# Four small changes of order and places in a streaming hybrid layer: column loads called earlier, SP's queue in program order in the heads, a third buffer, and own places for a row scale

## The chip, the cores and the metric

The kernel runs on one core of one Trainium2 chip. The metric is the device time of one execution in microseconds (us). A core has a matrix engine (PE, with the loading of its weights shown as PEld), a vector engine (DVE), a scalar engine (ACT), GpSimd (POOL) and SyncE (SP), which here issues nearly all DMA transfers. Each engine works through its own instructions in order and waits for the others by semaphores.

## The reference

One streaming step of one layer, for 512 frames of a new stream and 64 frames of a running one (576 rows, width 2048). All numbers are float32.

```
hn   = rmsnorm(x, g_norm1)
q, k, v, gb, gc, hc = split(hn @ w_in)            # six blocks of 1024 columns
q, k = rmsnorm per head                            # 8 heads x 128
o_attn = stick_breaking(q, [cached k, k], [cached v, v])   # strictly causal
u      = gc * hc
o_conv = gb * (causal convolution of width 3 over [state, u])   # 8 groups x 128 channels
mix    = concat(rmsnorm(o_attn), rmsnorm(o_conv))
x      = x + mix @ w_out
h2     = rmsnorm(x, g_norm2)
y      = x + (silu(h2 @ w_gate) * (h2 @ w_up)) @ w_down
```

The outputs are y of both streams, their new keys and values, and their new convolution states.

## The kernel before

**Tiling.** Activations lie transposed: channels on the 128 partitions, the 576 rows in the free dimension, in two halves of 288. A float32 value is split into a high and a low part (`split`, L222: ACT casts the high part, L223; DVE subtracts it, L224), and each product is three matmuls of 128 x 128 by 128 x 288. A weight is loaded by SP into one of the two slots of the tile `raw_a` (L184, or L946 for the columns below), then split in the same way (L176 and L177, or L223 and L224).

**The pipeline of ticks.** `project` (L489) runs one projection of 128 output columns: 16 steps for each of two halves, and one call of `pipe.tick()` after each step. Side work is written as generators that are spawned into this pipeline; each `yield n` asks to be resumed n ticks later. So the text order of the program, on every engine, is set by the ticks. A scheduler may then still change the order within each engine; inside `tc.manual_schedule(engines={SP})` SP's instructions stay in program order. Before the change this mode is on only in the later part of the conv products (L1112).

**Heads.** `head(h)` (L794) runs the projections of q, k and v for one head. It loads the cached keys and values (cK L798, cV L799), and spawns their transposition (L790), the scores (z, L672), softmax-like steps on ACT and the stores of new keys (ktok, L704) and values (vtok, L779).

**x_sums** (L570) is spawned after head 0. For each of 8 pieces it loads two tiles of x (L584), scales them on ACT (L587, L588), adds and subtracts on DVE (L590 and L592 among them), splits the sums into `xs_out` (L223, L224), and stores them to `xs_dram` on SP (L581). Its yields add up to 74 ticks a piece. The sums are the operands of a seven-product scheme for 2 x 2 block products (seven products in place of eight), used in the conv units and later.

**The first two conv groups** (`conv_group`, L889, for g below STD = 2) use three plain projections each: gc, hc, gb. During these, `head_forms` (L519) makes the seven combinations ("forms") of the attention output, splits them (hf) and stores them (`form_dram`, L544). Before the last projection, gb of group 1, `call_columns(range(3))` asks for the first three column loads of the conv units: two into the slots of raw_a, one into raw_c. `conv_prepare(0, 1)` and `conv_prepare(0, 2)` then split the first (whl).

**The conv units** run seven products p_ for each unit in the order of the list `corder` (`conv_run`, L990 for the matmuls). Two of the products are kept: `kept` (L997) copies a PSUM bank to a tile `part` with ACT (L999), in the tags "ms", "t" or "acc". A finished result goes through `done`: for a unit of kind "o" (the output projection's attention half, over the forms) DVE adds the bank to x (L1007), for the others cv is scaled (L1013, L1015).

**The mixed values.** `put_mix` (L510) scales a group's conv output by its gain into `mx` (ACT L513, DVE L515), sums squares (L507, L508), and POOL stores mx to `mix_dram` (L517). mx lies in the tag "hl", which has two buffers.

**The row scale.** `group_scale` (L558) splits the summed squares (`sqg`, also in "hl"), adds over channels with two matmuls (ssg, L470 and L471), and calls `rsqrt_mean` (L457), whose intermediate tiles ms and t have the tags "ms" and "t" with one buffer each.

**The output units' start.** In `open_out` three generators are spawned: `load_rest` (loads x from xt_dram on SP, L1070), `state_out` (PE transposition L1080, cst on ACT L1082, two stores L1083 and L1084) and `group_scale`. The forms are loaded by `load_forms` (L1054).

The projection of the mixed values and the feed-forward part after that (`out_proj` and on) take most of the time and are not touched.

Of the kernel before, what the change touches and what calls it, by code (L numbers as in the profile page):

```python
# [10 lines left out]
F32 = mybir.dt.float32  # L11
F32R = mybir.dt.float32r
# [4 lines left out]
P = 128  # L17
# [3 lines left out]
HALF = T // 2  # L21
HALVES = ((0, HALF), (HALF, T))
# [17 lines left out]
STD = 2  # L40
# [54 lines left out]
def tile_hybrid_stream_step(  # L95
# [99 lines left out]
    def next_weight():  # L195
        i = pos[0]
        pos[0] += 1
        end = first_out if i < first_out else first_block
        while len(raws) < min(i + 2, end):
            load_weight()  # L200
        while len(ready) < min(i + 2, end):
            split_weight(nc.gpsimd if i == 2 else nc.vector)
        while len(raws) < min(i + 3, end):
            load_weight()
        out = ready[i]
        ready[i] = None
        return out
# [18 lines left out]
    def parts(name):  # L226
        t = tmp.tile([P, 2, HALF], F32R, tag="hl", name=name)
        return t[:, 0], t[:, 1]
# [145 lines left out]
    with tc.manual_schedule(engines={mybir.EngineType.Activation, mybir.EngineType.DVE, mybir.EngineType.SP}):  # L374
        raw, raw3, src = weight_raw(0)
# [78 lines left out]

    hpool.release()

    def rsqrt_mean(dst, src, n, width):  # L457
        ms = tmp.tile([P, HALF], F32, tag="ms", name="ms", bufs=1)[:, :width]
        y = tmp.tile([P, HALF], F32, tag="y", name="y")[:, :width]
        t = tmp.tile([P, HALF], F32, tag="t", name="t", bufs=1)[:, :width]  # L460
        nc.vector.tensor_scalar(out=ms, in0=src, scalar1=1.0 / n, scalar2=EPS, op0=ALU.mult, op1=ALU.add)
        nc.scalar.activation(out=y, in_=ms, func=AF.Ln)
        nc.scalar.activation(out=y, in_=y, func=AF.Exp, scale=-0.5)
        nc.vector.tensor_tensor(out=t, in0=y, in1=y, op=ALU.mult)
        nc.vector.scalar_tensor_tensor(out=t, in0=t, scalar=-0.5, in1=ms, op0=ALU.mult, op1=ALU.mult)
        nc.vector.scalar_tensor_tensor(out=dst, in0=t, scalar=1.5, in1=y, op0=ALU.add, op1=ALU.mult)
# [19 lines left out]
                                op0=ALU.mult)  # L486
    split_weight(nc.vector)

    def project(evac, banks=(None, None), defer=None):  # L489
        whi, wlo = next_weight()  # L490
        for bank, (a, b) in zip(banks, HALVES):
            if bank:
                ps = ps_z.tile([P, 512], F32, tag=bank, name="pjz")[:, :HALF]
            else:
                ps = ps_pj.tile([P, HALF], F32, tag="pj", name="pj")
            product(ps, whi, wlo, slice(0, P), x_two, KD, a // HALF)
            if defer is None:
                evac(ps, a, b)
            else:
                defer.append((evac, ps, a, b))  # L500

    def add_squares(acc, src, first):
        if first:
            nc.scalar.activation(out=acc, in_=src, func=AF.Square)
        else:
            sq = tmp.tile([P, HALF], F32, tag="sq", name="sqm")
            nc.scalar.activation(out=sq, in_=src, func=AF.Square)  # L507
            nc.gpsimd.tensor_tensor(out=acc, in0=acc, in1=sq, op=ALU.add)  # L508

    def put_mix(g, i, src, gcol, acc, first):  # L510

        t = tmp.tile([P, 2, HALF], F32R, tag="hl", name="mx")
        nc.scalar.activation(out=t[:, 0], in_=src, func=AF.Copy, scale=gcol)  # L513
        add_squares(acc, src, first)
        nc.vector.scalar_tensor_tensor(out=t[:, 1], in0=src, scalar=gcol, in1=t[:, 0].bitcast(F32),  # L515
                                       op0=ALU.mult, op1=ALU.subtract)
        nc.gpsimd.dma_start(out=mix_dram[i, g].rearrange("f p t -> p f t"), in_=t.bitcast(F32))  # L517
# [39 lines left out]

    def group_scale(acc, dst, rows_of):  # L558

        for a, b in HALVES:  # L560
            sh, sl = parts("sqg")
            split(sh, sl, acc[:, a:b])
            yield rows_of
            ss = channel_sums(sh, sl, a, b, "ssg")
            rsqrt_mean(dst[:, a:b], ss, 8 * P, HALF)
            yield rows_of

    acc_a = rpool.tile([P, T], F32, tag="R", name="acc_a", bufs=2)
# [1 line left out]
    def x_sums():  # L570


        raw = o_half[1][:, 2:4, :]
        four = raw.rearrange("p k (i t) -> p (k i) t", i=2)
        b11, b12, b21, b22 = (four[:, q, :] for q in range(4))
        stt, tt = nc.vector.scalar_tensor_tensor, nc.vector.tensor_tensor

        def put(two, names):
            split(xs_out[:, :, 0, :], xs_out[:, :, 1, :], two)
            for r, q in enumerate(names):  # L580
                nc.sync.dma_start(out=xs_dram[q, j].rearrange("f p t -> p f t"), in_=xs_out[:, r].bitcast(F32))  # L581

        for j in range(NP):
            nc.sync.dma_start(out=raw, in_=xt_dram[2 * j : 2 * j + 2].rearrange("k p t -> p k t"))  # L584
            yield 18
            ge, go = g1c[:, 2 * j : 2 * j + 1], g1c[:, 2 * j + 1 : 2 * j + 2]
            nc.scalar.activation(out=b11, in_=b11, func=AF.Copy, scale=ge)  # L587
            nc.scalar.activation(out=b22, in_=b22, func=AF.Copy, scale=go)  # L588
            yield 8
            stt(out=b11, in0=b12, scalar=ge, in1=b11, op0=ALU.mult, op1=ALU.subtract)  # L590
            yield 8
            stt(out=b12, in0=b12, scalar=ge, in1=b22, op0=ALU.mult, op1=ALU.subtract)  # L592
            yield 8
            put(four[:, 0:2, :], (0, 2))
            yield 8
            tt(out=b22, in0=b22, in1=b11, op=ALU.subtract)
            yield 8
            stt(out=b21, in0=b21, scalar=go, in1=b22, op0=ALU.mult, op1=ALU.subtract)
            yield 8
            put(four[:, 2:4, :], (3, 1))  # L600
            yield 8
        free_places.append(True)
# [191 lines left out]
    def head(h):  # L794
# [26 lines left out]
        project(v_evac, ("z2", None) if h == 0 else (None, None))  # L821
        pipe.spawn(values(h, st, Ev))

    for h in range(NH):
        head(h)
        if h == 0:
            pipe.spawn(x_sums())


    cstate = rpool.tile([P, 2, 2, NG], F32, name="cstate")  # L830
# [15 lines left out]
        nc.sync.dma_start(out=t.bitcast(F32), in_=xs_dram[q].rearrange("j f p t -> p j f t"))  # L846

    def open_units():
        cx = apool.tile([P, 1024 + UW], F32, tag="ob", name="cx")
        bt["s1"] = cx[:, :1024].rearrange("p (j c) -> p j c", c=P)  # L850
        bt["c"] = cx[:, 1024 : 1024 + UW - 2]

# [11 lines left out]
    def put_u(a, b, x, y):  # L864
        e = min(b, TP)
        nc.vector.tensor_tensor(out=u[:, a + 2 : e + 2], in0=x[:, : e - a], in1=y[:, : e - a], op=ALU.mult)
        if b > TP:
            nc.vector.tensor_tensor(out=u[:, TP + 4 :], in0=x[:, e - a :], in1=y[:, e - a :], op=ALU.mult)
# [19 lines left out]
    def conv_group(g):  # L888
        gates = []  # L889

        def evac_gc(ps, a, b):
            t = tmp.tile([P, HALF], F32, tag="sq", name="gcr")
            nc.vector.tensor_tensor(out=t, in0=ps, in1=R1[:, a:b], op=ALU.mult)
            nc.vector.tensor_tensor(out=t, in0=t, in1=R1[:, a:b], op=ALU.mult)
            gates.append(t)

        project(evac_gc)
        begin_u(g)
        project(lambda ps, a, b: put_u(a, b, ps, gates[a // HALF]))

        def evac_gb(ps, a, b):
            if not bt:
                open_b()
            if a == 0:
                end_u(g)
            t = tmp.tile([P, HALF], F32, tag="y", name="gbr")
            nc.vector.tensor_tensor(out=t, in0=ps, in1=R1[:, a:b], op=ALU.mult)
            put_o(g, a // HALF, t)

        if g == STD - 1:  # L910
            call_columns(range(3))
            for p_ in (1, 2):
                conv_prepare(0, p_)
        project(evac_gb)
# [11 lines left out]
    def call_columns(gone):  # L926
        cfree.extend(gone)
        while cwanted:
            n, c = cwanted[0]
            place = [q for q in cfree if c is not None or q < 2][:1]  # L930
            if not place:
                return
            cwanted.pop(0)
            q = place[0]
            cfree.remove(q)
            raw = bt["raw"] if q == 2 else raw_tile["A"][:, q, :]
            if c is None:
                d = CU[n][1]
                nc.sync.dma_start(out=raw.rearrange("p (k c) -> p k c", c=2 * P),
                                  in_=w_out[:AW, 2 * d * P : 2 * (d + 1) * P].rearrange("(k p) c -> p k c", p=P))  # L940
                v = raw.rearrange("p (j s h c) -> p j s h c", s=2, h=2, c=P)
                for c in range(2):
                    cregion[n, c] = q, v[:, :, 0, c, :], v[:, :, 1, c, :]
            else:
                c0 = cstart[c + 2 * (CU[n][0] == "b")] + CU[n][1] * P
                nc.sync.dma_start(out=raw.rearrange("p (k c) -> p k c", c=P),  # L946
                                  in_=w_in[:, c0 : c0 + P].rearrange("(k p) c -> p k c", p=P))
                v = raw.rearrange("p (j s c) -> p j s c", s=2, c=P)
                cregion[n, c] = q, v[:, :, 0, :], v[:, :, 1, :]
# [800 lines left out]
```

## Time and profile before

| | us |
|---|---|
| median of three runs | 2415.28 |
| the three runs | 2414.83, 2415.28, 2418.58 |
| the profiled execution's own time | 2414.43 |
| its span in the profile | 2412.7 |
| PE busy | 2377.6 (99%) |
| DVE busy | 1910.5 (79%) |
| ACT busy | 1166.6 (48%) |
| POOL busy | 294.6 (12%) |

A row of the timeline has the start of an instruction in us, its duration in us, the engine, the line of the program, the operation, what it writes <- what it reads, the shape, and how many of one kind follow each other (x24); in brackets stands how long the engine had been idle before it and what released it. SPq rows are transfers being issued; they have the time that the issuing took. A row of the windows has the stretch, its length, the busy time and number of instructions of PE, PEld, DVE, ACT and POOL, then the granted PE clock as a share of full speed, the mean busy share of the 16 DMA engines (it can read a little over 1), and GB/s. A row of the groups has line, engine, operation, tiles, shapes and count, then busy time and mean ns of one, then the idle time before them and what ended it. A row of the transfers ends with the median us from issue to landing. Matmuls overlap their neighbours by a little, so a series of them is best timed from start to start.

### The profile page before, as it was taken

How to read it: one execution, taken by the hardware profiler on the slowest of the kernel's cores; microseconds unless marked ns; L12 is line 12 of the kernel's file. 1: busy time of each engine (PE TensorE's matmuls, PEld its weight loads, DVE VectorE, ACT ScalarE, POOL GpSimd, SP SyncE). 2: the span in 40 equal slices, each digit the busy share in tenths (PEclk: the TensorE clock that was granted, in tenths of full speed). 3: DMA queues.
4: the chain of work that ended last, by engine and by line, in shares of the span. 5: the costliest groups of instructions: out<-in, count | busy, mean ns of one | idle time of the engine just before them, and what ended most of it. 6: DMA issues, size and time to landing. Idle time of an engine off the chain costs nothing.

```text
span 2412.7 us, 44204 instructions
## 1 busy us (share of the span) xinstructions
PE 2377.6 (99%) x17825; PEld 2363.1 (98%) x17825; DVE 1910.5 (79%) x2862; ACT 1166.6 (48%) x2091; POOL 294.6 (12%) x400
## 2 busy tenths in 40 slices
PE   8999999999999999999999999999999999999999
PEld 8999999989999999999999999999999999999999
DVE  7777666678888768888888888888888877887875
ACT  6666555434434445444444444444444444444444
POOL 1111111231112220000000000000000001431211
PEclk9999999999999999999999999999999999999999
DMA  8554322584367432544444444434534945885642
GB/s 269 166 179 147 89 72 85 179 285 120 90 205 265 141 136 92 163 150 134 140 145 149 135 134 149 154 115 154 159 117 149 328 147 181 237 233 196 198 132 80
DMA packets 504085, 386.05 MB, mean 160 GB/s; under 512 B 11854, under 2 KB 493000, under 8 KB 503880
## 3 DMA queue, kind: packets, MB, share of 16 engines
q1 hardware_dynamic: 496712, 371.40, 48.2%
q0 software_dynamic: 6448, 11.51, 2.1%
q8 instruction: 139, 2.28, 0.4%
q14 instruction: 66, 0.54, 0.1%
q10 hardware_dynamic: 720, 0.33, 0.0%
HBM read 296.47 MB, written 86.72 MB: 159 GB/s over the span
## 4 chain that ended last, share of the span: by engine, by line
PE 79%; DVE 10%; DMA 5%; ACT 3%; issue 2%; POOL 1%; SPq 0%; ACTq 0%; DVEq 0%; POOLq 0%
PE psy L1500 33%; PE psw L1500 16%; PE pj L214 8%; PE psx L1500 8%; PE pjo L214 4%; DVE whl L224 3%; PE psy L990 2%; DMA raw_a<-in_w_in_dram 2%; PE pw L1343 2%; PE psw L990 1%; DVE wlo L177 1%; PE psx L990 1%; DMA raw_c<-in_w_in_dram 1%; DMA xs_dram<-xs_out 1%; DMA x<-xt_dram 1%
## 5 line engine op out<-in xcount | busy, mean ns | idle before, releaser
L224 DVE TENSOR_TENSOR whl<-raw_a,whl 128x1024 fp32r<-128x1024 f32 (+4 forms) x372 | 393.1, 1058 | 66.2 <-ACT whl L223 65.0
L1500 PE MATMUL psy<-t,whl 128*128 128x288 f32 x2916 | 437.9, 295 | 0.0
L1500 PE MATMUL psy<-h_s,whl 128*128 128x288 f32 x2724 | 411.2, 295 | 1.8 <-ACT part L1510 1.8
L223 ACT CAST whl<-raw_a 128x1024 fp32r<-128x1024 f32 (+4 forms) x372 | 326.6, 880 | 160.1 <-issue 37.6
L1500 PEld LDWEIGHTS psy<-t,whl 128*128 128x128 f32 x2916 | 403.4, 188 | 0.2
L214 PE MATMUL pj<-x,whi 128*128 128x288 f32 x1856 | 397.7, 299 | 0.3 <-DVE x L357 0.3
L1500 PEld LDWEIGHTS psy<-h_s,whl 128*128 128x128 f32 x2724 | 377.9, 188 | 2.3 <-ACT part L1510 2.2
L1500 PE MATMUL psw<-t,whl 128*128 128x288 f32 x2592 | 376.8, 295 | 0.0
L1500 PEld LDWEIGHTS psw<-t,whl 128*128 128x128 f32 x2592 | 354.1, 188 | 0.2
L214 PEld LDWEIGHTS pj<-x,whi 128*128 128x128 f32 x1856 | 306.8, 189 | 1.0 <-DVE x L357 0.6
L214 PE MATMUL pj<-x,wlo 128*128 128x288 f32 x928 | 274.5, 296 | 0.1
L224 DVE TENSOR_TENSOR whl<-raw_b,whl 128x1024 fp32r<-128x1024 f32 (+5 forms) x186 | 196.3, 1056 | 69.8 <-ACT whl L223 68.6
L223 ACT CAST whl<-raw_b 128x1024 fp32r<-128x1024 f32 (+5 forms) x186 | 160.8, 867 | 163.6 <-issue 69.8
L1510 ACT COPY part<-psy 128x288 f32<-128x288 f32 x237 | 94.7, 400 | 266.2 <-PE psy L1500 266.1
L214 PEld LDWEIGHTS pj<-x,wlo 128*128 128x128 f32 x928 | 175.2, 189 | 0.7 <-DVE wlo L424 0.3
L1500 PE MATMUL psx<-h_s,whl 128*128 128x288 f32 x1122 | 165.0, 295 | 0.0
L1500 PEld LDWEIGHTS psx<-h_s,whl 128*128 128x128 f32 x1122 | 154.2, 188 | 0.0
L1263 POOL DMA_DIRECT2D hid_dram<-form x3 | 2.2, 726 | 976.4 <-DVE form L224 974.5
L223 ACT CAST whl<-s 128x1024 fp32r<-128x1024 f32 (+5 forms) x79 | 70.1, 888 | 98.9 <-PE psw L1500 97.4
L177 DVE TENSOR_TENSOR wlo<-raw_a,whi 128x1024 fp32r<-128x1024 f32 (+1 forms) x80 | 97.6, 1234 | 11.2 <-ACT whi L176 7.5
L214 PE MATMUL pjo<-mixc,whi 128*128 128x288 f32 x512 | 101.7, 294 | 0.0
L176 ACT CAST whi<-raw_a 128x1024 fp32r<-128x1024 f32 (+1 forms) x85 | 85.6, 1023 | 20.1 <-PE pjo L214 9.0
(442 smaller groups left out, 3985.4 us busy)
## 6 DMA issues: line engine op xcount, KB each, us to landing
hid_dram<-form SPq DMA_DIRECT2D x147, 288.0 KB, 2.6
raw_a<-in_w_in_dram SPq DMA_DIRECT2D x41, 1024.0 KB, 5.8
raw_a<-in_w_gate_dram SPq DMA_DIRECT2D x23, 1024.0 KB, 6.0
raw_a<-in_w_up_dram SPq DMA_DIRECT2D x23, 1024.0 KB, 5.6
raw_b<-in_w_gate_dram SPq DMA_DIRECT2D x21, 1024.0 KB, 6.6
raw_b<-in_w_up_dram SPq DMA_DIRECT2D x21, 1024.0 KB, 7.3
h_s<-hid_dram SPq DMA_DIRECT2D x10, 2016.0 KB, 10.0
raw_a<-in_w_out_dram SPq DMA_DIRECT2D x16, 1024.0 KB, 5.2
```

The costliest lines, as they stand in the source:

```text
L176: nc.scalar.copy(out=hi[:, a:b], in_=raw[:, a:b])
L177: lo_eng.tensor_tensor(out=lo[:, a:b], in0=raw[:, a:b], in1=hi[:, a:b].bitcast(F32), op=ALU.subtract)
L214: mm(ps, w_[:, k, csl], x_, start=(k == 0 and n == 0), stop=(k == nk - 1 and n == 2))
L223: nc.scalar.copy(out=hi, in_=src)
L224: (lo_eng or nc.vector).tensor_tensor(out=lo, in0=src, in1=hi.bitcast(F32), op=ALU.subtract)
L990: mm(ps, whl[:, w_, j, :], x_, start=(start and j == 0 and q == 0), stop=(j == m - 1 and q == 2), skip_group_check=True)
L1263: q.dma_start(out=hid_dram[fp][2 * n - 2 : 2 * n].rearrange("f p t -> p f t"), in_=t.bitcast(F32))
L1343: mm(pss[j, i], w_[:, k, j * P : (j + 1) * P], x_, start=(kk == 0 and k == 0 and n == 0), stop=(kk == 1 and k == 7 and n == 2))
L1500: mm(ps, whl[:, w_, j, :], x_, start=(start and j == 0 and q == 0), stop=(j == len(xs_) - 1 and q == 2), skip_group_check=True)
L1510: nc.scalar.copy(out=t, in_=st["y"])
```

## The change

Four things are changed.

1. `project` takes a function `then`, which it calls after it has fetched its weight. In the last of the two plain conv groups the first two column loads (raw_a) are called there, in the projection of hc, and only the third (raw_c) is called before the projection of gb.
2. SP's queue is in program order from the end of `head(0)` to the end of the heads.
3. In the conv units every third turn of `put_mix` uses a place of its own, at the end of the tile `cx`, which grows by 2 x 288 elements a partition. The other turns keep the two buffers of "hl".
4. `group_scale` takes the two pairs of sqg from one tile in the tag "uc" in place of "hl", and hands `rsqrt_mean` tiles in the tags "r" and "sq" (two buffers each) in place of "ms" and "t".

```diff
-    def rsqrt_mean(dst, src, n, width):
-        ms = tmp.tile([P, HALF], F32, tag="ms", name="ms", bufs=1)[:, :width]
+    def rsqrt_mean(dst, src, n, width, ms=None, t=None):
+        if ms is None:
+            ms = tmp.tile([P, HALF], F32, tag="ms", name="ms", bufs=1)[:, :width]
+            t = tmp.tile([P, HALF], F32, tag="t", name="t", bufs=1)[:, :width]
         y = tmp.tile([P, HALF], F32, tag="y", name="y")[:, :width]
-        t = tmp.tile([P, HALF], F32, tag="t", name="t", bufs=1)[:, :width]
...
-    def project(evac, banks=(None, None), defer=None):
+    def project(evac, banks=(None, None), defer=None, then=None):
         whi, wlo = next_weight()
+        if then:
+            then()
...
+    turns = {}
+
     def put_mix(g, i, src, gcol, acc, first):
 
-        t = tmp.tile([P, 2, HALF], F32R, tag="hl", name="mx")
+        turns["mx"] = turns.get("mx", 0) + 1
+        if "mx" in bt and turns["mx"] % 3 == 0:
+            t = bt["mx"]
+        else:
+            t = tmp.tile([P, 2, HALF], F32R, tag="hl", name="mx")
...
     def group_scale(acc, dst, rows_of):
 
-        for a, b in HALVES:
-            sh, sl = parts("sqg")
+        four = cpool.tile([P, 2, 2, HALF], F32R, tag="uc", name="sqg")
+        for i, (a, b) in enumerate(HALVES):
+            sh, sl = four[:, i, 0], four[:, i, 1]
             split(sh, sl, acc[:, a:b])
             yield rows_of
             ss = channel_sums(sh, sl, a, b, "ssg")
-            rsqrt_mean(dst[:, a:b], ss, 8 * P, HALF)
+            ms, t = (tmp.tile([P, HALF], F32, tag=tag, name=tag + "g") for tag in ("r", "sq"))
+            rsqrt_mean(dst[:, a:b], ss, 8 * P, HALF, ms, t)
             yield rows_of
...
+    head_mode = ExitStack()
     for h in range(NH):
         head(h)
         if h == 0:
             pipe.spawn(x_sums())
+            head_mode.enter_context(tc.manual_schedule(engines={mybir.EngineType.SP}))
+    head_mode.close()
...
-        cx = apool.tile([P, 1024 + UW], F32, tag="ob", name="cx")
+        cx = apool.tile([P, 1024 + UW + 2 * HALF], F32, tag="ob", name="cx")
+        bt["mx"] = cx[:, 1024 + UW :].rearrange("p (f t) -> p f t", t=HALF).bitcast(F32R)
...
         begin_u(g)
-        project(lambda ps, a, b: put_u(a, b, ps, gates[a // HALF]))
+        project(lambda ps, a, b: put_u(a, b, ps, gates[a // HALF]),
+                then=(lambda: call_columns(range(2))) if g == STD - 1 else None)
...
         if g == STD - 1:
-            call_columns(range(3))
+            call_columns([2])
             for p_ in (1, 2):
                 conv_prepare(0, p_)
```

## Prediction

> **What bounds the kernel now.** I read the page first, then PE's timeline stretch by stretch, looking only for idle time, and at each gap the timelines of the engine named as its releaser and of SP's queue.
>
> ```profile
> span 2412.7 us, 44204 instructions
> PE 2377.6 (99%) x17825; PEld 2363.1 (98%) x17825; DVE 1910.5 (79%) x2862; ACT 1166.6 (48%) x2091; POOL 294.6 (12%) x400
> ```
>
> PE is the bound: a gap in PE that is closed moves the end forward by its length, and nothing else does. The change leaves PE's instructions and their order alone; it adds no arithmetic anywhere. So its worth is the sum of the gaps that it closes less those that it opens, at five places. The gaps cost twice in some of them: the granted clock is lower for some us after two stalls close together.
>
> **(a) Head 0, the scores.**
>
> ```profile
> 70.73 0.67 ACT L223 CAST xs_out<-o_ob 128x576 fp32r<-128x576 f32 x1 [0.28 <-DVE o_ob L592]
> 72.43 0.38 PE L672 MATMUL z<-qh,kh 128*128 128x256 f32 x1 [1.82 <-ACT kh L223]
> 72.99 0.58 PE L672 MATMUL z<-qh,kl 128*128 128x256 f32 x1 [0.18 <-DVE kl L224]
> 77.35 0.38 PE L214 MATMUL pj<-x,whi 128*128 128x288 f32 x1
> 72.00:76.00 4.00, 3.40 (x11) 3.01 (x12) 1.82 (x4) 2.10 (x5) 0.00 (x0) 0.62 1.11 354
> 318.60 0.28 PE L672 MATMUL z<-qh,kh 128*128 128x256 f32 x1
> 321.44 0.38 PE L214 MATMUL pj<-x,whi 128*128 128x288 f32 x1
> ```
>
> PE waits 1.82 + 0.18 = 2.00 us for kh and kl. Ahead of kh in ACT's queue stands a step of x_sums, 0.67 us, and DVE has such steps ahead of kf. In the changed order, which is known before any run, every step of x_sums follows both halves of kh. That brings z forward by something between 0 and 1.82; I take 0.85, the row of 0.67 and a little for DVE. The scores themselves last 77.35 - 72.43 = 4.92 us here and 321.44 - 318.60 = 2.84 later: 2.08 us go to the granted clock of 0.62. With the stall more than halved I give the spell 0.6 to vanish: 1.25. Together -2.1 (bounds 0 and -4.1).
>
> **(b) Heads 1 and 2.** From one head's first score to the next:
>
> ```profile
> 115.63 0.38 PE L672 MATMUL z<-qh,kh 128*128 128x256 f32 x1 [0.43 <-ACT kh L223]
> 167.81 0.38 PE L672 MATMUL z<-qh,kh 128*128 128x256 f32 x1
> 219.68 0.28 PE L672 MATMUL z<-qh,kh 128*128 128x256 f32 x1
> 269.14 0.28 PE L672 MATMUL z<-qh,kh 128*128 128x256 f32 x1
> L223 ACT CAST xs_out<-o_ob 128x576 fp32r<-128x576 f32 x16 | 10.7, 672 | 6.9 <-DMA xs_dram<-xs_out 6.0 <-DVE o_ob L592 0.8
> ```
>
> 52.18, 51.87, then 49.46 us once x_sums is done: the two heads that carry it pay 2.72 + 2.41 = 5.13. ACT also stood 6.0 us, in order, until an earlier store of xs_out had landed. With SP's queue in program order the eight pieces no longer run ahead; by their yields (74 ticks each) they last until head 7, about 1.3 pieces a head instead of 2.7. If each piece costs the same wherever it runs, nothing is won; if the thinner stream fits into ACT's gaps, all 5.13 is. I take -2.0, nearer to the first end, since heads 3 to 7 now get steps that they did not have (bounds +2 and -5.1).
>
> **(c) Start of the conv units.**
>
> ```profile
> 506.26 0.29 PE L214 MATMUL pj<-x,whi 128*128 128x288 f32 x1
> 508.32 0.40 PE L990 MATMUL psy<-x,whl 128*128 128x288 f32 x1 [1.77 <-ACT whl L223]
> 509.58 4.85 PE L990 MATMUL psy<-x,whl 128*128 128x288 f32 x23 [0.86 <-DVE whl L224]
> 522.14 3.44 PE L990 MATMUL psx<-x,whl 128*128 128x288 f32 x24 [1.33 <-DVE cv L1013]
> 525.42 3.33 PE L990 MATMUL psy<-xs_t,whl 128*128 128x288 f32 x24
> 528.59 3.33 PE L990 MATMUL psw<-xs_t,whl 128*128 128x288 f32 x24
> 550.89 1.34 PE L990 MATMUL psy<-x,whl 128*128 128x288 f32 x9
> 484.15 16.34 SPq L544 DMA_DIRECT2D form_dram<-hf  x15
> 500.54 3.19 SPq L946 DMA_DIRECT2D raw_a<-in_w_in_dram  x2
> 507.23 1.99 ACT L223 CAST whl<-raw_a 128x1024 fp32r<-128x1024 f32 x2 [3.03 <-DMA raw_a<-in_w_in_dram]
> 513.22 2.00 ACT L223 CAST whl<-raw_c 128x1024 fp32r<-128x1024 f32 x2 [3.23 <-DMA raw_c<-in_w_in_dram]
> 537.66 1.23 DVE L958 TENSOR_TENSOR cx<-raw_a 128x1024 f32<-128x1024 f32 x1 [6.27 <-DMA raw_a<-in_w_in_dram]
> ```
>
> A product of 24 matmuls lasts 528.59 - 525.42 = 3.17 us. The last projection's rows end at 506.55; the first four products take until 525.42, 18.87 us for 4 x 3.17 = 12.68, a loss of 6.19. The cause is in SP's queue: the first two column loads leave at 500.54 behind form stores, land under load, and ACT splits them only at 507.23. In the changed order they follow the 12th form store instead of the 23rd and are split while the last projection still runs. The 15 stores of the row at 484.15 are the 9th to the 23rd, 1.09 us each; so the loads leave near 488.5, 12 us sooner. Then the 1.77 and 0.86 go, with the slow spell behind them (the 23 matmuls at 509.58 lasted 4.85, where 24 last 3.33), and DVE's splits leave the crowded stretch, which should free cv too. What is late next is the third load, raw_c: it stays behind 23 stores, and its split, now at 513.22, feeds the third product, which PE would reach at 506.55 + 6.34 = 512.89. With 2 MB less ahead of it, it should land sooner, but not by much: I leave 1.0 of the 6.19, so -5.2 (bounds -2 and -6.2). The 16 form stores that the two loads now stand in front of can be held until raw_a's slots are free; what reads the forms comes with the output units, so only the tiles they are written from could be free late. ACT's scaling of uc moves too, ahead of the last six casts of forms, and POOL's copies of the state with it, under the same cover. I cost both at nothing (if it held xs_t's load, up to the whole second loss below). The next seven products lose 550.89 - 525.42 - 7 x 3.17 = 3.28, since the fourth column load lands at 537.66 behind other transfers. This load leaves when DVE has split what it overwrites, and so moves forward with PE, but the transfers ahead of it do so only in part: -0.8 (bounds +1 and -3.3).
>
> **(d) Start of the output units.** Here a gap closes and the time does not come back.
>
> ```profile
> 718.57 1.35 PE L990 MATMUL psx<-forms,whl 128*128 128x288 f32 x9
> 722.86 1.87 PE L990 MATMUL psy<-forms,whl 128*128 128x288 f32 x12 [2.43 <-ACT part L999]
> 728.34 6.57 PE L990 MATMUL psy<-forms,whl 128*128 128x288 f32 x36 [1.99 <-ACT part L999]
> 735.00 1.86 PE L990 MATMUL psw<-forms,whl 128*128 128x288 f32 x12
> 726.89 0.43 ACT L223 CAST sqg<-acc_c 128x288 fp32r<-128x288 f32 x1 [3.56 <-DMA mix_dram<-mx]
> 721.21 4.14 SPq L1070 DMA_DIRECT2D x<-xt_dram  x2
> 733.53 0.46 DVE L1007 TENSOR_TENSOR x<-psx,x 128x288 f32<-128x288 f32 x1 [0.26 <-DMA x<-xt_dram]
> 720.00:724.00 4.00, 1.57 (x12) 1.33 (x11) 3.04 (x7) 2.17 (x5) 2.85 (x4) 1.00 1.07 387
> ```
>
> mx and sqg share two buffers, and ACT stands 3.56 us at 726.89 until a store of mix has landed; the copy of part behind it holds PE. The change gives every third mx and sqg places of their own, so both stalls (2.43 + 1.99) should go, and with them the slow spell: 36 matmuls took 735.00 - 728.34 = 6.66 instead of 4.76, 1.90 more. That is 6.32 us of PE. But the product at 735.00 also needs a PSUM bank that DVE empties right after 733.53, when x has landed, 12.3 us after its issue, with the DMA engines full (share 1.07). Nothing in the change makes these bytes fewer or their start earlier, so PE will arrive at about 728.7 and wait there until 735.0. The gain is 0, and a stall of 6.3 us may bring a slow spell of its own of 1.90: I take half, +1.0 (bounds +1.9 and -3).
>
> **(e) End of the row scale.**
>
> ```profile
> 810.92 1.86 PE L990 MATMUL psy<-forms,whl 128*128 128x288 f32 x12 [2.39 <-ACT part L999]
> 813.27 0.67 PE L990 MATMUL psy<-forms,whl 128*128 128x288 f32 x3 [0.49 <-ACT part L999]
> ```
>
> part shares its tag with the t of rsqrt_mean, and its copies stand behind ACT's weight splits. With tags of its own the first copy moves ahead of two splits, but the second now stands behind them. Of 2.88 I take -1.3 (bounds 0 and -2.9).
>
> **The sum.** -2.1 - 2.0 - 5.2 - 0.8 + 1.0 - 1.3 = -10.4 us. The profiled execution took 2414.43, of which the span is 2412.7; it becomes 2404.0. The median of three runs, 2415.28, lies 0.85 above that execution, so I predict 2404.9.
>
> [...]
>
> **The rivals.**
>
> *The clock answers only to long stalls* (0.1). What it would do here: the spells in (a) and (c) have another cause and stay, and the 6.3 us stall of (d) gets the whole 1.90. (a) gives 0.85; in (c) the spell, 4.85 - 3.33 x 23/24 = 1.66, stays, so -3.5; then -0.85 - 2.0 - 3.5 - 0.8 + 1.9 - 1.3 = -6.55, 2408.7. For it: the 2.39 us alone at 810.92 are followed by 1.86 for 12 matmuls, no slow spell. Against it: three slow spells, each right behind two stalls. [...]
>
> *Little is won* (0.16). DMA bounds the start of the conv units as it does (d): raw_c lands no earlier, so (c) gives only -2; (a) -0.85, (b) 0, (d) +1.9, (e) 0: about -1, 2414.3. For it: three loads in this stretch end a wait of ACT or DVE. Against it: SP's queue, not the transfer, held the first two.
>
> *Slower: SP's program order stalls ACT* (0.12).
>
> ```profile
> 106.33 0.37 SPq L184 DMA_DIRECT2D raw_a<-in_w_in_dram  x1
> 125.15 0.37 SPq L799 DMA_DIRECT2D cV<-in_cache_v_dram  x1
> 139.75 1.04 ACT L176 CAST whi<-raw_a 128x1024 fp32r<-128x1024 f32 x1
> raw_a<-in_w_in_dram SPq DMA_DIRECT2D x41, 1024.0 KB, 5.8
> ```
>
> A head's load of cV waits for the head before it to finish with cV (125.15). Today the weight load at 106.33 overtakes it; then it cannot, nor can the stores of xs_out. The weight is safe: about 125.5 + 5.8 = 131.3, split at 139.75, 8.4 to spare. But a held store holds the next xs_out on ACT, and the softmax behind that. If every one of heads 1 to 7 pays what head 1 pays now and 1 us more, 3.7 each, that is 25.9 in place of 5.13; with -8.4 from the rest, +12.4: 2427.7. It is slower than no change from 1.93 us a head. Against it: the waits of x_sums are spread 1.3 pieces to a head.
>
> **The numbers.** The forecast has 0.62. The range reaches from the joint better half of the bounds to just past "little is won": 2398 to 2416. Below about 0.2%, 4.8 us, a measurement of this kernel can't tell from no change. Faster: forecast 0.62 and the clock rival 0.1, 0.72; same 0.16; slower 0.12. That the change does not take effect is no case of its own: the changed order shows all four parts.
>
> **What will show it.** After: no stall by whl at the first conv product and raw_a issued near 488; z of head 0 near 71.5 at clock 1.00; heads 1 to 7 nearly equal, under 51 us; one stall of about 6 us before the first psw product of the output units, ended by DVE L1007; part's stalls in (e) about half. I am wrong if heads 3 to 7 exceed 51 us, or if the raw_c split holds the third conv product for over 2 us.

## The result, and the profile after

The changed kernel takes 2409.21 us (median of 12 runs, 2407.25 to 2411.66); the kernel before, run beside it, 2414.54 (12 runs, 2411.22 to 2418.58). The ratio is 0.9977, with a 95% interval of 0.9968 to 0.9986: faster by 5.3 us, where 10.4 were forecast. The profiled execution took 2407.78 us.

From the page and PE's timeline of the changed kernel (its lines stand 1 to 16 further down than in the kernel before: L1006 is L990, L1015 is L999, L683 is L672):

```profile
span 2406.1 us, 44221 instructions
PE 2375.1 (99%) x17825; PEld 2363.2 (98%) x17825; DVE 1911.9 (79%) x2862; ACT 1166.1 (48%) x2091; POOL 293.9 (12%) x400
...
69.22 0.39 PE L683 MATMUL z<-qh,kh 128*128 128x256 f32 x1 [0.81 <-ACT kh L223]
110.48 0.39 PE L683 MATMUL z<-qh,kh 128*128 128x256 f32 x1
163.25 0.28 PE L683 MATMUL z<-qh,kh 128*128 128x256 f32 x1
213.31 0.28 PE L683 MATMUL z<-qh,kh 128*128 128x256 f32 x1
257.62 0.40 PE L472 MATMUL ss<-sq,oner 128*128 128x288 f32 x1 [1.87 <-DVE sq L224]
266.50 0.28 PE L683 MATMUL z<-qh,kh 128*128 128x256 f32 x1
503.76 3.33 PE L1006 MATMUL psy<-x,whl 128*128 128x288 f32 x24
510.10 0.29 PE L1006 MATMUL psy<-x,whl 128*128 128x288 f32 x1
514.44 4.78 PE L1006 MATMUL psy<-x,whl 128*128 128x288 f32 x23 [4.04 <-DVE whl L224]
522.23 3.33 PE L1006 MATMUL psy<-xs_t,whl 128*128 128x288 f32 x24
545.21 9.68 PE L1006 MATMUL psy<-x,whl 128*128 128x288 f32 x72
710.97 1.75 PE L1006 MATMUL psy<-forms,whl 128*128 128x288 f32 x12
723.99 7.38 PE L1006 MATMUL psy<-forms,whl 128*128 128x288 f32 x36 [6.10 <-DMA forms<-form_dram]
731.21 1.75 PE L1006 MATMUL psw<-forms,whl 128*128 128x288 f32 x12
807.00 0.67 PE L1006 MATMUL psy<-forms,whl 128*128 128x288 f32 x3 [0.79 <-ACT part L1015]
```

PE executes the same matmuls in the same order (17825 in both), so the two traces can be set against each other from one matmul to the same one later:

| stretch | before | after | difference | forecast |
|---|---|---|---|---|
| start to kc of head 0 | 61.78 | 59.62 | -2.16 | none |
| kc to the scores of head 1 | 53.85 | 50.86 | -2.99 | (a) -2.1 |
| scores of head 1 to those of head 4 | 153.51 | 156.02 | +2.51 | (b) -2.0 |
| on to the last plain projection's end | 237.41 | 237.41 | 0.00 | 0 |
| first four conv products | 18.87 | 18.32 | -0.55 | (c) -5.2 |
| next seven | 25.47 | 22.98 | -2.49 | (c) -0.8 |
| on to the first product over the forms | 166.10 | 165.76 | -0.34 | none |
| start of the output units, to the psw product | 18.01 | 20.24 | +2.23 | (d) +1.0 |
| on to the mixed values' projection | 81.83 | 79.36 | -2.47 | (e) -1.3 |
| the rest, to PE's last row | 1591.03 | 1590.63 | -0.40 | 0 |

The first row is not put down to the change: 1.68 of its 2.16 us stand already at PE's 51st matmul (14.99 in place of 16.67 us), ahead of anything that the change touches, and the other kernels below reach kc after 59.15 to 60.72 us. Without it the profile shows -4.5. In the table one sees an old stall leave and another come in three places: the stall by kh is less than half (0.81 us, with a granted clock of 1.00 from 68 to 76 us), but from the scores of head 3 to those of head 4 (213.31 to 266.50) it takes 53.19 us in place of 49.46, with a stall of 1.87 in head 4's k projection; the first conv product starts without a gap at 503.76, but the third waits 4.04 us; the two stalls by part are gone at the output units, but one of 6.10 us by the forms has come.

### The profile page after: what moved, and what is told of

Same layout as the page of the kernel before. It is cut to its first block, busy times and chain, and to the rows that moved or that the text cites. A ratio compares the mean times of both kernels' runs of the same rounds, so it can differ in the third digit from the quotient of the medians.

```text
span 2406.1 us, 44221 instructions
## 1 busy us (share of the span) xinstructions
PE 2375.1 (99%) x17825; PEld 2363.2 (98%) x17825; DVE 1911.9 (79%) x2862; ACT 1166.1 (48%) x2091; POOL 293.9 (12%) x400
## 4 chain that ended last, share of the span: by engine, by line
PE 84%; DVE 8%; DMA 4%; ACT 2%; issue 1%; POOL 0%; SPq 0%; ACTq 0%; DVEq 0%; POOLq 0%
PE psy L1516 33%; PE psw L1516 16%; PE pj L214 12%; PE psx L1516 8%; PE pjo L214 4%; DVE whl L224 3%; PE psy L1006 2%; PE pw L1359 2%; DMA raw_a<-in_w_in_dram 1%; PE psw L1006 1%; PE psx L1006 1%; DMA raw_c<-in_w_in_dram 1%; DMA forms<-form_dram 1%; PE z L683 1%; ACT whl L223 0%
```

## Experiments

Each kernel is the changed one with the edit shown. The stage lengths are those of the table, from one profiled execution each. Executions of the same code differ: the long last stretch, which no edit touches, took 1590.4 to 1593.6 us. So a stage is trusted further than a difference of 2 us in the time. The profiled execution is not always a middle one: that of e1 was its slowest (2413.50, median 2409.52), that of e11 among its fastest (2410.39, median 2413.34).

### The conv units' start

**Part 1 undone (e2).**

```diff
-                then=(lambda: call_columns(range(2))) if g == STD - 1 else None)
+                then=None)
-            call_columns([2])
+            call_columns(range(3))
```

> The changed kernel with all three column loads called before the projection of gb again (part 1 undone). Theory: what part 1 won at the first conv product (6.2 us) was lost again at the third (5.8 us, raw_c's split), and its net gain, about 3 us, lies in the fourth column load of 527 to 545 us. So about +3 us against the changed kernel, near 2412, with the stalls at the first product back and none by raw_c at the third. Rival: part 1 brings nothing at all, since the transfers of this stretch are the limit: within 1 us of the changed kernel.

2412.98 us, ratio 0.9989 (0.9980 to 0.9998): 3.8 above the changed kernel's median, 2.9 by the ratios. The old picture is back: the first four products 18.76 us, the next seven 25.74 in place of 22.98. The two intervals overlap, so the time alone does not show a loss; the stages do, and they agree with those of the kernel before (18.87 and 25.47). Part 1 is worth 3 us, and nearly all of it lies in the second stretch.

**raw_c earlier (e4).**

```diff
                 bt["raw"] = apool.tile([P, 2048], F32, tag="oa", name="raw_c")
+                call_columns([2])
...
-            call_columns([2])
```

> The changed kernel with the third column load (raw_c) called as soon as its place is free, behind 14 form stores and not behind 23. Theory: the changed kernel waits 4.04 us at the third conv product for raw_c's split and runs 1.6 us slow after it; with raw_c some 8 us earlier its splits are done before DVE's sums of the first two columns, and both go: -5 to -5.6 us, near 2404. Rival 1: the DMA engines are full from 488 us on, so raw_c lands only 2 to 3 us earlier: -2. Rival 2: the form stores that now wait behind the load hold xs_t's load, and a stall of the same size appears at 522 to 535 us: 0.

2410.58 us, ratio 0.9980 (0.9971 to 0.9989): no gain. The second rival had forecast 0, but by a stall at 522 to 535 us, and none came there (the next seven products took 22.96 us). In the changed kernel ACT's and DVE's timelines show the third product's operand:

```profile
485.17 4.50 SPq L962 DMA_DIRECT2D raw_a<-in_w_in_dram  x2
500.32 0.50 SPq L962 DMA_DIRECT2D raw_c<-in_w_in_dram  x1
508.55 2.00 ACT L223 CAST whl<-raw_c 128x1024 fp32r<-128x1024 f32 x2 [2.38 <-DMA raw_c<-in_w_in_dram]
511.10 1.23 DVE L978 TENSOR_TENSOR raw_a<-raw_a 128x1024 f32<-128x1024 f32 x1
513.17 2.96 DVE L224 TENSOR_TENSOR whl<-raw_c,whl 128x1024 fp32r<-128x1024 f32 x2
```

raw_c is cast from 508.55 on, but DVE first makes the sums of the columns that came early (L974 to L978) and splits raw_c at 513.17. With raw_c issued 7.5 us sooner, PE stood 2.75 + 3.25 = 6.00 us in place of 4.04, in two pieces, but with no slow spell behind either (23 matmuls in 3.30 us, 24 in 3.45), and the first four products took 19.07 us against 18.32:

```profile
492.80 0.56 SPq L962 DMA_DIRECT2D raw_c<-in_w_in_dram  x1
513.04 3.30 PE L1006 MATMUL psy<-x,whl 128*128 128x288 f32 x23 [2.75 <-DVE whl L224]
519.59 3.45 PE L1006 MATMUL psx<-x,whl 128*128 128x288 f32 x24 [3.25 <-DVE cv L1029]
```

**DVE in program order too (e7).**

```diff
+    dve_mode = ExitStack()
+    dve_mode.enter_context(tc.manual_schedule(engines={mybir.EngineType.DVE}))
     for p_ in (1, 2):
         conv_prepare(1, p_)
...
+        if k_ == 3:
+            dve_mode.close()
```

> The kernel with raw_c called early (e4), and DVE besides in program order from the preparation of the second unit to the fourth conv product, which puts the split of raw_c ahead of the sums of the first two columns. Theory: not the transfers but DVE's order sets the third product, and after it the fourth: in e4 the split followed two of the sums (1.2 us each), and the rest of them held cv. Then the first four products take about 13 to 14 us in place of 18.3: -4.5 against the changed kernel, near 2405. Rival: DVE has too much work in this stretch in any order; the sums come later, and the stall moves to the fifth product, which needs them: -1 or less.

2411.75 us, ratio 0.9992 (0.9984 to 1.0001), the first four products 21.13 us. The theory's 13 to 14 us did not come. The split of raw_c was in time, and the wait went to the fourth product, not to the fifth as the rival had it:

```profile
510.15 3.30 PE L1006 MATMUL psy<-x,whl 128*128 128x288 f32 x23 [0.40 <-DVE whl L224]
518.76 5.79 PE L1006 MATMUL psx<-x,whl 128*128 128x288 f32 x24 [5.32 <-DVE cv L1029]
```

Neither the landing of raw_c nor the place of its split is the cause by itself. The windows of the changed kernel from 484 to 524 us sum up to

```profile
sum 40.00, PE 35.96 PEld 35.72 DVE 36.30 ACT 18.94 POOL 19.41; mean PE 3.60 PEld 3.57 DVE 3.63 ACT 1.89 POOL 1.94
```

and DVE is as busy as PE. (In the kernel before the same 40 us have DVE busy for 35.08.)

**Less work for DVE (e9).**

```diff
         if p_ == 6:
...
-            tt(out=s1, in0=st["a21"], in1=st["a22"], op=ALU.add)
...
+            if n:
+                tt(out=s1, in0=st["a21"], in1=st["a22"], op=ALU.add)
...
+            else:
+                st["s1"] = st["a21"]
-        if p_ == 3:
+        if p_ == 3 and n:
```

> The changed kernel without the four sums of the first conv unit's columns (the three of L974 to L976 and that of L978, 1.2 us each on DVE); the unit's products then use the plain columns, so that part of the computation is left out. Theory: at the start of the conv units DVE is the bound in any order (36 of 40 us busy from 484 to 524 in the changed kernel); with 4.9 us of its work taken away the third product's stall (4.0 us) and the slow spell behind it go nearly: the first four products take 13 to 14.5 us in place of 18.3, -4 to -5. Rival: raw_c's landing (508.5 in the changed kernel) decides; ACT and DVE then need 2.2 us more, the third product starts near 511 and at most 0.8 us are lost, so this rival gives the same here, but it can't give what e4 and e7 showed. A third: the order of DVE's work alone; then nothing is left of the stall, but a stall by cv as in e7 appears at the fourth product, and the four take 16 or more.

This kernel leaves out four sums, so it tells of the time alone. The first four products took 13.62 us: the stall of the third and its slow spell are gone (granted clock 1.00 from 504 to 536 us), and none came at the fourth, so it is DVE's work in this stretch that PE waits for. But the next seven took 26.97 in place of 22.98, and the time is 2408.09 (ratio 0.9976, 0.9967 to 0.9985). Of 4.7 us, 4.0 were given back in the next seven products. The reason stands in DVE's timeline, in the wait for the fourth column load. First the changed kernel, then this one:

```profile
524.77 4.21 SPq L962 DMA_DIRECT2D raw_a<-in_w_in_dram  x2
531.89 1.22 DVE L974 TENSOR_TENSOR cx<-raw_a 128x1024 f32<-128x1024 f32 x1 [3.68 <-DMA raw_a<-in_w_in_dram]
```

```profile
519.42 7.34 SPq L962 DMA_DIRECT2D raw_a<-in_w_in_dram  x2
529.88 1.23 DVE L975 TENSOR_TENSOR cx<-raw_a 128x1024 f32<-128x1024 f32 x1 [7.75 <-DMA raw_a<-in_w_in_dram]
536.80 3.31 PE L1009 MATMUL psy<-xs_t,whl 128*128 128x288 f32 x23 [1.15 <-DVE whl L224]
```

Counted from the last projection's end, that load is there after 31.1 us before the change (537.66 less 506.55), after 28.0 with it, and after 27.4 here. PE's first eleven products take 44.34, 41.30 and 40.59 us: each time they end 13.2 to 13.3 us behind that landing. The 3 us that part 1 wins are the 3 us by which the fourth load comes sooner. It is hardly issued sooner, 20.85 us after the projection's end in place of 21.39 (and 21.29 in e2, where it lands after 31.2 again), so the gain is a shorter time from issue to landing (7.1 us in place of 9.7). That this is because 2 MB left the crowded time (DMA share 1.15 and 1.11 from 508 to 516 us before the change) fits, and was not tried by itself. In e9 it was issued 4.0 us sooner than in the changed kernel, and landed only 0.6 sooner.

What PE does before that is cover, but only down to a second limit, which the changed kernel has just reached: four products in 18.32 and seven more in 22.97 us end at 41.29, the load and what follows it at 27.97 + 13.24 = 41.21. In e1 the load was there after 26.7 us, the seven took 22.99 all the same, and the end came 14.0 us behind the landing. By these sums neither less work for DVE nor a sooner load would pay much alone from here on.

### The output units' start

**Parts 3 and 4 undone (e3).**

```diff
-        if "mx" in bt and turns["mx"] % 3 == 0:
+        if False:
...
-            sh, sl = four[:, i, 0], four[:, i, 1]
+            sh, sl = parts("sqg")
...
-            rsqrt_mean(dst[:, a:b], ss, 8 * P, HALF, ms, t)
+            rsqrt_mean(dst[:, a:b], ss, 8 * P, HALF)
```

> The changed kernel with mx and sqg in the two shared buffers again, and the row scale's ms and t in the shared tags (parts 3 and 4 undone). Theory: at the start of the output units the transfers decide, so the two stalls by part come back (2.4 + 2.0 us and a slow spell of 1.9) and the one of 6.1 us by the forms, with its spell of 2.5, goes: about 2 us better there, 2.4 us worse at the end of the row scale, near 2409 to 2410 in all. Rival: the transfers only happened to be late in the profiled execution of the changed kernel; then undoing costs 6 + 2.4, near 2417.

2410.87 us, ratio 0.9982 (0.9972 to 0.9991).

```profile
715.38 2.70 PE L1004 MATMUL psy<-forms,whl 128*128 128x288 f32 x12 [2.20 <-ACT part L1013]
721.98 4.99 PE L1004 MATMUL psy<-forms,whl 128*128 128x288 f32 x36 [1.64 <-DMA forms<-form_dram]
727.12 1.86 PE L1004 MATMUL psw<-forms,whl 128*128 128x288 f32 x12
```

The stretch starts at 709.72 here, so the psw product comes after 17.40 us; in the changed kernel after 20.24, with the forms there after 13.02 in place of 12.26. One of the two stalls by part is back (2.20 us); in the place of the second PE waits for the forms, 1.64 us. The stalls by part were cover for the transfer, as the theory had it: without them PE waits for it in one piece, and pays the slow clock behind it (0.50 from 724 to 728 us in the changed kernel). Of the 2.84 us between the two, 0.76 are the later forms and 2.08 the 36 matmuls behind them (7.22 us in place of 5.14). It is more than the spread: the kernels of this document with the own places and the forms in the old order take 19.2 to 21.1 us here, those without the places 17.4, 18.0 (the kernel before) and 18.6 (e8). The end of the row scale is 2.34 us longer again (from ssg to pjo 12.28 in place of 9.94).

**Only the row scale's tags kept (e8).** (The first two hunks of the diff above.)

> The changed kernel with mx and sqg in the two shared buffers again, but the row scale's ms and t in tags of their own (of parts 3 and 4 only that is kept). Theory: the own places of mx and sqg bring nothing at the start of the output units, where the forms' landing decides, and cost a slow spell behind the single long stall: -2 to -2.7 there; the 2.35 us at the end of the row scale come from the tags and stay: near 2406.5. Rival: sqg's own place is what brings the 2.35; then the time is that of e3, which was within 1.7 us of the changed kernel.

2407.89 us, ratio 0.9975 (0.9965 to 0.9985). The row scale's end stays short (9.92), so it is the tags and not sqg's place that bring the 2.35. From the first product over the forms to pjo it takes 98.13 us against 99.60; the kernels with the places and the forms in the old order take 98.5 to 100.5, so the places for mx and sqg cost 0.4 to 2.4 us there by these profiles, and the time does not show it (0.9975 against 0.9977).

**Form 4 loaded last (e5).**

```diff
-            if p_ == 7:
+            if p_ == 4:
                 load_forms(apool.tile([P, NH // 2, 2, HALF], F32R, tag="oa", name="forms0"), 0, 4)
```

> The changed kernel with the load of form 4 (1152 KB, the last one needed of the seven) called behind those of forms 5 and 3 and not ahead of them. Theory: at the start of the output units PE waits 6.1 us for form 5 because the DMA engines work through all that was called before it; with one transfer less ahead of it the wait falls by about 2.9 us (1152 KB at the 390 GB/s of this stretch), and the slow spell behind it may shorten: -3 to -5 against the changed kernel, near 2405 to 2406, unless form 4 or x then ends a wait of its own (-0 to -1 in that case). Rival: the places of mx and sqg hold PE in some other way there; then the wait stays at 6 us and the time at 2409.

2407.33 us, ratio 0.9973 (0.9962 to 0.9984).

```profile
717.34 2.91 PE L1006 MATMUL psy<-forms,whl 128*128 128x288 f32 x20 [1.73 <-DMA forms<-form_dram]
721.33 1.83 PE L1006 MATMUL psy<-forms,whl 128*128 128x288 f32 x12 [0.55 <-DMA forms<-form_dram]
726.11 2.35 PE L1006 MATMUL psw<-forms,whl 128*128 128x288 f32 x12 [2.95 <-DVE x L1023]
```

6.10 us became 1.73 + 0.55, and then came 2.95 by x: the wait that the prediction had named stood right behind. The stretch is 2.63 shorter than with the change, but the one after it 1.63 longer, and the time does not show the gain of 3 to 5 us that the theory had.

**Form 4 behind x too (e12).**

```diff
+        if (n, p_) == (NCU, 1):
+            load_forms(apool.tile([P, NH // 2, 2, HALF], F32R, tag="oa", name="forms0"), 0, 4)
```

> The kernel of e5 with form 4 called still later, behind the first two tiles of x too. In e5 the 6.1 us by the forms had become 1.7 and 0.6 us by the forms and 2.95 us by DVE's addition to x, which waits for x to land. Theory: the bytes decide: x lands 2.5 to 3 us sooner, form 4 by as much as x's two tiles later (1.5 us), and the same product then waits for form 4: the stretch from the first product over the forms to the product at 735.0 of the kernel before takes 16 to 17.6 us (17.6 in e5, 20.2 in the changed kernel), the time is within 1.5 us of e5's 2407.3. Rival: the order among the last of these transfers decides; then the 2.95 go, 2404.5.

2405.22 us, ratio 0.9971 (0.9961 to 0.9982), the stretch 16.90 us. The psw product now waits 2.54 for form 4 in place of 2.95 for x, as the theory had it: the bytes decide, and the wait that the rival had gone has stayed, though the time is nearer to the rival's 2404.5. It has the lowest ratio of all, but its interval overlaps that of the change; that it beats the changed kernel is not shown.

**Both: tags only, and form 4 last (e10).**

```diff
-        if "mx" in bt and turns["mx"] % 3 == 0:
+        if False:
...
-            sh, sl = four[:, i, 0], four[:, i, 1]
+            sh, sl = parts("sqg")
...
-            if p_ == 7:
+            if p_ == 4:
```

> The kernel of e8 (mx and sqg in the shared buffers, own tags for the row scale) with form 4 called last (e5): the version that the runs so far point to. Theory: at the start of the output units the transfers up to the first two tiles of x decide, whatever the rest does; so the gains of e5 and e8 don't add up: about 2407, within 1 us of either. Rival: they add up: -1.9 and -1.3 against the changed kernel's 2409.2, near 2406.

2410.48 us, ratio 0.9983 (0.9974 to 0.9992). They don't add up; it is no better than either, and 3 us above the 2407 that was expected.

### The heads

**Part 2 undone (e1).**

```diff
-            head_mode.enter_context(tc.manual_schedule(engines={mybir.EngineType.SP}))
```

> The changed kernel with SP's queue left to the scheduler again in the heads (part 2 undone), the other parts kept. Theory: each part acts at its own place. Then head 0's score stall is 1.8 us again with a slow clock behind it (about 3 us), heads 1 and 2 cost some 5 us more than the later ones, and the stall of 1.87 us at 255 us of the changed kernel, with its slow spell (3.7 us together), is gone: 3 + 5 - 2 (what the changed kernel's heads 1 to 3 still pay) - 3.7, about +1 to +2 us against the changed kernel, near 2410 to 2411. Rival: the stall at 255 has nothing to do with SP's order and stays: +5 to +6, near 2414 to 2415.

2409.52 us, ratio 0.9978 (0.9970 to 0.9987): the same time as with it. From kc of head 0 to the scores of head 4 it takes 208.71 us here, 207.36 before the change and 206.88 with it; the other kernels with SP in program order and x_sums untouched took 204.6 to 207.2. The stall by kh is back (2.00 us), the one at 257 is gone. So the order may win some 2 us in these stages, and nothing that the time can show. All of that lies ahead of head 1's scores: from kc to there it takes 54.03 us here and 53.85 before the change, against 50.5 to 51.5 in the kernels in program order with x_sums untouched. From there to the scores of head 4 it takes 154.68 here and 153.51 before, against 153.5 to 156.0: no gain, and no loss beyond the spread.

Some rows say more of these heads. The first three are of the changed kernel (ACT's casts in x_sums, then PE in head 1's stretch), the last two show that place of PE in the kernel before:

```profile
L223 ACT CAST xs_out<-o_ob 128x576 fp32r<-128x576 f32 x16 | 10.7, 671 | 14.1 <-DMA xs_dram<-xs_out 12.9 <-DVE o_ob L603 1.1
118.88 1.06 PE L780 MATMUL os<-ws,cV 128*128 128x128 f32 x8
120.84 0.33 PE L653 MATMUL ktb<-ident,kf 128*128 128x128 f32 x1 [0.68 <-ACT o_oa L781]
124.06 1.05 PE L769 MATMUL os<-ws,cV 128*128 128x128 f32 x8
126.02 0.33 PE L642 MATMUL ktb<-ident,kf 128*128 128x128 f32 x1 [0.68 <-ACT o_oa L770]
```

ACT's idle time until an earlier store of xs_out had landed is 12.9 us in program order (11.6 to 14.8 in the kernels with it), 6.0 before and 6.7 in e1. And head 1's stretch holds ten matmuls of head 0's output (os) more than the later heads' stretches; with the wait behind them they take 1.96 us, before the change and after it.

**Other yields in x_sums (e6).**

```diff
-            yield 18
+            yield 24
...
-            yield 8
+            yield 7
```

> The changed kernel with other yields in x_sums: 24 ticks behind the load and 7 at each later place in place of 18 and 8 (73 a piece in place of 74). Theory: in head 4 (the fifth) the steps of one piece fall on the end of the k projection, ahead of DVE's split of sq, and PE waits there; that is a matter of the phase between 74 ticks a piece and 96 a head. With other phases the 2.3 to 3.8 us that this head pays go, or move to another head, and the heads' sum changes by up to 4 us. Rival: the stall comes from the load of x that SP issues late; then 6 more ticks behind the load cure it wherever it would fall, and all heads from the fourth on take 49.5 us: -2.5 to -3.5.

2409.93 us, ratio 0.9983 (0.9974 to 0.9992).

```profile
256.85 0.40 PE L472 MATMUL ss<-sq,oner 128*128 128x288 f32 x1 [1.13 <-DVE sq L224]
376.55 0.33 PE L653 MATMUL vtb<-ident,Ev 128*128 128x128 f32 x1 [2.55 <-ACT ktok L654]
```

From the scores of head 3 to those of head 4 it takes 50.92 in place of 53.19 us (51.6 to 53.6 in the other kernels in program order with x_sums untouched), and from those of head 6 to those of head 7 52.18 in place of 49.46. The stall moves with the phase between the pieces (73 ticks) and the heads (96), as the theory had it; a longer lead for the load does not cure it.

**Work of x_sums on POOL (e11).**

```diff
-            split(xs_out[:, :, 0, :], xs_out[:, :, 1, :], two)
+            split(xs_out[:, :, 0, :], xs_out[:, :, 1, :], two, nc.gpsimd)
...
-            tt(out=b22, in0=b22, in1=b11, op=ALU.subtract)
+            nc.gpsimd.tensor_tensor(out=b22, in0=b22, in1=b11, op=ALU.subtract)
```

> The changed kernel with the low parts of xs_out (0.75 us each on DVE, 16 of them) and one of the four sums of a piece on POOL in place of DVE. Theory: in the heads with SP in program order x_sums costs what DVE and ACT steps it puts ahead of a head's own; with 2 us a piece less on DVE the stall of head 4 (DVE's split of sq late by 1.9, a slow spell behind it) goes: that head takes 49.5 to 50.5 us in place of 51.6 to 53.6, and the time falls by 2 to 3.5. Rival: POOL takes 1.5 to 2 us for a split of this size; stores and the next piece then come later, and the stall moves (to ktok or kh on ACT): 0.

2413.34 us, ratio 0.9994 (0.9985 to 1.0003): worse than the changed kernel, where the rival had no change. POOL's splits took 1.64 us each, within the rival's price. The stretch to the scores of head 4 got no shorter (53.74 us), and a new stall came ahead of head 1's, by DVE's sq and not by ktok or kh:

```profile
106.44 0.40 PE L472 MATMUL ss<-sq,oner 128*128 128x288 f32 x1 [1.83 <-DVE sq L224]
```

## Why the prediction was right, and where it was too large

The direction and the range (2398 to 2416) held, and the sum was twice too large. That it was no worse is partly luck: in the profile the five places together give -3.76 of the -10.4, and the other -2.9 lie in stretches of which the prediction said nothing, mostly the start. Both signs by which it wanted to be called wrong came: one of heads 3 to 7 exceeds 51 us (53.19), and raw_c's split holds the third conv product for 4.04 us. So (b) and (c) failed by its own measure. By its steps:

- **(a)** right. -2.1 forecast, -2.99 in the table, and e1, in the old order, has the old length again; the stall by kh fell from 1.82 to 0.81 us, by 1.01, near the 0.85 taken off, and the slow spell went (granted clock 1.00; from z to the next projection 3.25 us in place of 4.92).
- **(b)** wrong: -2.0 forecast, +2.51 in the profile, just outside its bound of +2. By all the profiles it is nothing, within the spread. Two steps failed. The price: 5.13 us were put down to x_sums, but 1.96 of head 1's 2.72 are head 0's os and the wait behind it, which no order removes. And the overlap, that a thinner stream of x_sums fits into the gaps: with 3, 2 and 3 of its 16 casts, in place of 6, 5 and 0, the stretches of heads 1 to 3 took 52.77, 50.06 and 53.19 us. It did fit in those of heads 4 and 5, which took 49.45 and 49.46 us with 2 and 3 casts. The run of e6 shows that the stall moves with the phase, so the number of casts does not decide; what does was followed no further.
- **(c)** right in sign and mis-sized: -6.0 forecast for its two terms, -3.04 measured (part 1's worth by e2: 2.9). The failed step is "I leave 1.0 of the 6.19". raw_c's split was named as next in line, but at 1.0 us; with its slow spell (23 matmuls in 4.78 us, granted clock 0.78 and 0.79 from 512 to 520 us) it cost 5.6, as DVE makes sums ahead of it. The second term was the real one: -0.8 forecast, -2.49 measured, the sooner fourth load, and e9 shows that this load decides the stretch when DVE is relieved.
- **(d)** right as a mechanism: a 6 us stall takes the place of the two, ended by a transfer. It was the forms (6.10 us) and not x; e5 shows x right behind. The slow spell came whole (36 matmuls in 731.21 - 723.99 = 7.22, 2.5 more than the 4.76), so +2.23 in place of +1.0. The half was the mis-sized term.
- **(e)** right as a mechanism, too small: -2.35 (e8) in place of -1.3. The first copy moved ahead of ACT's splits, as forecast, and PE's 2.39 us before it went altogether. The second does stand behind two of them, also as forecast, but PE waits only 0.79 us for it (0.49 before). The mis-sized term is that second wait:

```profile
804.65 2.00 ACT L176 CAST whi<-raw_a 128x1024 fp32r<-128x1024 f32 x2 [0.61 <-PE psw L1006]
806.56 0.39 ACT L1015 COPY part<-psy 128x288 f32<-128x288 f32 x1
```

The time lies near that of the first rival, 2408.7, but not for its reason: the spells of (a) and (c) did leave with their stalls, and new ones came with new stalls. The rival "little is won" had the transfers as the reason for (c), which holds for the fourth load; raw_c, which it named, landed 2.0 us sooner (4.6 us after the projection's end in place of 6.6). Its gain was too small. The slower rival's mechanism is there, since ACT's waits for stores of xs_out went from 6.0 to 12.9 us, but the heads did not pay its 3.7 us each: one of seven did (with the stall at 257.62, which DVE's sq ends and no store).

## What to carry to other kernels

Where PE waits for something early in a stretch, look for the transfer or the engine whose work ends that stretch, before the stall is priced: stalls ahead of it are cover, and closing them moves the wait. Here 3 of 6 us came back at the conv units and none of 6 us at the output units, and only the wait with little behind it (the row scale's tags) paid nearly in full, 2.35 of 2.88 us. Before a difference between two stretches is called the price of some side work, count the matmuls in both. An experiment that takes the suspected work away altogether, as e9 did with DVE's sums, shows in one run both that the suspect was the cause and who is next.

## What the runs showed of the hardware

The lowered clock does not need two stalls, as I had read the rows of the kernel before. In the changed kernel's windows, after one stall of 1.87, one of 4.04 and one of 6.10 us:

```profile
256.00:260.00 4.00, 2.38 (x12) 2.38 (x13) 4.00 (x10) 1.17 (x4) 0.89 (x1) 0.78 0.00 0
512.00:516.00 4.00, 1.56 (x6) 1.56 (x7) 3.96 (x6) 2.72 (x5) 0.80 (x1) 0.78 0.32 86
724.00:728.00 4.00, 4.00 (x17) 4.00 (x18) 0.00 (x0) 0.76 (x2) 0.00 (x0) 0.50 1.06 402
```

Nor does the length decide among the short ones: after 2.75 us (e4, at 513.04) 23 matmuls took 3.30, no spell, and 3.25 at 519.59 had none (24 in 3.45), and after 2.39 (810.92, before the change) there was none either (granted clock 1.00 from 811 to 815 us), while 1.87 had one (0.78). Nor does the place in the program: the stall of 1.86 to 1.87 us in head 4's k projection was followed by a spell of 1.6 us in the changed kernel, e4, e7 and e8, and by none in e2, e3, e5 and e12, where that stretch took 51.6 to 51.9 us in place of 53.2 to 53.6. The stalls of 3.43 to 6.76 us behind the first 60 us of these runs all had one. What decides whether a stall has one was not tried.
